# Reading the stored sums of a fast matrix product through GpSimd's transfer queue in place of SyncE's

## The chip, the core and the metric

The kernel runs on one core of a Trainium2 chip. A core has five engines with instruction streams of their own: TensorE (PE), VectorE (DVE), ScalarE (ACT), GpSimd (POOL) and SyncE (SP). Any of SP, ACT and POOL can issue transfers; the transfers themselves run on 16 DMA engines that the core's queues share. The metric is the device time of one launch in microseconds (us), lower being better.

## What is computed

One block of a streaming encoder, in float32, over 512 tokens of width 2048. The reference, cut to what matters:

```python
h = rms_norm(x, norm_gain)
proj = jnp.einsum('bsd,de->bse', h, w_in)
(sb_q, sb_k, sb_v, sb_g, gl_q, gl_k, gl_v, gl_g, gl_lr) = jnp.split(proj, offsets, axis=-1)

a_out = stick_breaking_attention(rms_norm(q) * gq, rms_norm(k) * gk, v)     # 8 heads of 128
a_out = from_heads(rms_norm(a_out) * go) * jax.nn.silu(sb_g)

log_alpha = jax.nn.log_sigmoid(gl_lr @ gla_w_alpha + gla_b_alpha) / 16
b_out = gated_linear_attention(gl_q, gl_k, gl_v, log_alpha)                # 4 heads, chunks of 64
b_out = from_heads(rms_norm(b_out) * ggo) * jax.nn.silu(gl_g)

x = x + jnp.concatenate([a_out, b_out], axis=-1) @ w_out
```

Most of the arithmetic is in the two projections, `h @ w_in` (2048 x 7184) and `mixed @ w_out` (2048 x 2048).

## The kernel before

**Products.** The projection's columns are cut into groups of 512. A float32 product is made of three matmul passes over a high and a low part of each factor (`hi`, `lo`): high by high, low by high, high by low. `split` makes the two parts of a weight tile, the high one on ACT (L177) and the low one on DVE (L178). The first two groups (q, k) are multiplied directly (`direct`). All others go two at a time through `pair`, which does seven block products in place of eight by the scheme of Strassen and Winograd: the left factor (tokens by inner dimension) is cut into two halves each way, and so are the weights. The pairs come in the order qv, vk, gqk, gv, ga, gb, o0, o1; the last two belong to `w_out`.

**The left factor.** `Acts` holds it, once for `h` (tiles named `_h`) and once for `mixed` (`_m`). Its seven forms are A11, D, NQ, S4, A12, S3 and A22, each in four slices u = 0 to 3 of the inner dimension. One slice of one form, high and low part together, is a tile of 128 partitions by 1024 numbers, 512 KB. D and S3 stay in SBUF. The other five forms are made once, written to DRAM (`_write`, L263, tiles `far_*`), and read again by `get` (L253) in every later pair, into one of four buffers (tag `as`, `NAS` = 4). There are 132 such reads: 12 in qv and 20 in each of vk, gqk, gv, ga, gb and o1. In the trace A11, A12 and A22 all bear the name `A_h` (`A_m`), NQ is `NQ_h` and S4 is `S_h`; D and S3 are kept tiles, though S3 also bears the name `S_h`.

**The four stages of a pair.** Each has four slices u. The first multiplies A11 and D (weights `st_..a`, L170, and `pw_..`). The second multiplies NQ and S4 (weight `st_..b`). The third loads two weight tiles, c and d, multiplies A12 by c and S3 by `d`, a difference that DVE makes in place (L183) and of which ACT makes the high part `hi_..d`; behind that, `gather` (L188) adds a further weight block to `pw` in SBUF by a transfer that POOL issues. The fourth splits the gathered sum (`hi_..e`) and multiplies A22 by it.

**What sets the order.** Each engine runs its instructions in program order. PE's order is written out by hand: the products of a pair with the steps of attention and of the gated part (`side.step()`) between them. The other engines' order comes from a scheduler that takes what is `urgent()` first and otherwise goes by buffers: weight tiles `st` have three buffers, `pw` four. Every weight load (L170), every read of a stored sum (L253), every write of one (L263) and every load of the residual rows `xr` (L494) is issued by SP, in one line. POOL issues the 32 gathers and does the masks of attention (L866, L873, L770). The output's residual additions are on DVE (L503, L512).

Of the kernel before, what the change touches and what calls it, by code (L numbers as in the profile page):

```python
# [7 lines left out]
F32 = mybir.dt.float32  # L8
# [85 lines left out]
def body(ctx: ExitStack, tc: tile.TileContext, x, xT, w_in, w_lr, w_alpha, vecs, w_out, out):  # L94
    nc = tc.nc
# [30 lines left out]
    def ut(name, dt=F32):  # L126

        held[0] += 1
        assert held[0] <= NU4, name
        return ring.tile([P, 2, S], dt, name=name, tag="u4", bufs=NU4)  # L130
# [10 lines left out]
    def urgent():  # L141
        return tc.high_priority(offset=URGENT)
# [47 lines left out]
    class Acts:  # L190
# [50 lines left out]
        def get(self, f, u):  # L241
            key = (f, u)
            if key in self.kept:
                return self.kept[key]
            name = f"{f}_{self.tag}{u}"
            with urgent():
                if f in self.keep:
                    t = ut(name, F32R).rearrange("p h (k t) -> p h k t", k=KU)
                    self.kept[key] = t
                else:  # L250
                    t = work.tile([P, 2, KU, H2], F32R, name=name, tag="as", bufs=NAS)
                    if key in self.far:
                        nc.sync.dma_start(t.bitcast(F32), self.far[key])  # L253
                        return t
                self._split(t, f, u)
                if f not in self.keep:
                    self._write(t, f, u, name)
            return t
# [848 lines left out]
```

## Time and profile before

| what | value |
|---|---|
| median of three runs (lowest, highest) | 921.23 us (918.57, 922.48) |
| the profiled execution: its time, its span | 920.89 us, 918.9 us |
| mean granted clock of TensorE, share of full speed | 0.966 |
| PE, DVE, ACT, POOL busy | 829.1, 665.4, 481.3, 68.4 us |
| bytes moved by transfers | 216.98 MB, 236 GB/s |

The profile is of one execution; the span runs from its first instruction to its last. Busy time leaves out the instructions that only issue transfers or wait, except on POOL, where the issue of a transfer is an instruction of its own. The granted clock is what the chip let TensorE have.

### The profile page before, as it was taken

What the parts mean: (1) busy time and instruction counts of PE and PEld (TensorE: products, weight loads), DVE (VectorE), ACT (ScalarE), POOL (GpSimd) and SP (SyncE); (2) the same over time, 40 slices, a digit from 0 to 9 for tenths busy, and PEclk for the clock granted to TensorE, in tenths of its full rate; (3) what the DMA queues carried; (4) which work ended last, traced back from release to release, by engine and by line L of the source; (5) the groups of instructions that cost most, each with busy time, mean ns of one, the idle gap of its engine ahead of it and who ended that gap; (6) DMA issues with size and microseconds to landing.
All of it is one profiled execution on the core that took longest, in us unless ns stands there. A gap on an engine that the chain in (4) does not pass through costs nothing.

```text
span 918.9 us, 11502 instructions
## 1 busy us (share of the span) xinstructions
PE 829.1 (90%) x4082; PEld 692.7 (75%) x4082; DVE 665.4 (72%) x821; ACT 481.3 (52%) x822; POOL 68.4 (7%) x113
## 2 busy tenths in 40 slices
PE   8899999899898589897999999989996989876988
PEld 5688878688787489897787788877774867665866
DVE  4542987678878987779855776778956999764654
ACT  5464566366776757564653445545734845432322
POOL 1000000100221100220100000000001000100000
PEclk9999999999999989999999999999997999897999
DMA  8878328994487524885459953887489548997695
GB/s 297 307 277 295 115 92 297 303 351 147 164 265 237 205 93 153 251 248 219 138 158 304 353 192 115 251 256 291 164 303 284 190 160 302 315 391 253 228 341 139
DMA packets 62041, 216.98 MB, mean 236 GB/s; under 512 B 7040, under 2 KB 7168, under 8 KB 61984
## 3 DMA queue, kind: packets, MB, share of 16 engines
q1 hardware_dynamic: 54928, 195.26, 59.0%
q0 software_dynamic: 4608, 16.78, 10.1%
q10 hardware_dynamic: 2448, 4.21, 1.2%
q8 instruction: 32, 0.52, 0.2%
q14 instruction: 25, 0.20, 0.1%
HBM read 191.06 MB, written 25.17 MB: 235 GB/s over the span
## 4 chain that ended last, share of the span: by engine, by line
PE 24%; DMA 13%; DVE 9%; issue 3%; ACT 2%; DVEq 0%; SPq 0%; ACTq 0%
PE x_o L111 4%; PE x_gb L111 3%; PE y_o L111 3%; PE y_gv L111 3%; PE x_gv L111 2%; DMA st_gbc<-in_w_in 2%; PE x_ga L111 2%; PE y_gb L111 2%; PE y_ga L111 2%; DMA st_o1d<-in_w_out 2%; DMA st_gad<-in_w_in 1%; DMA pw_o<-in_w_out 1%; DMA st_o0c<-in_w_out 1%; PE o L111 1%; DMA xr<-in_x 1%
## 5 line engine op out<-in xcount | busy, mean ns | idle before, releaser
L111 PE MATMUL z_q<-hi_q,A_h 128*128 128x512 f32 x128 | 35.5, 431 | 6.8 <-DVE A_h L291 3.3
L111 PEld LDWEIGHTS z_q<-hi_q,A_h 128*128 128x128 f32 x128 | 26.5, 210 | 15.4 <-DVE A_h L291 4.2
L111 PE MATMUL z_k<-hi_k,A_h 128*128 128x512 f32 x128 | 30.6, 391 | 0.0
L111 PEld LDWEIGHTS z_k<-hi_k,A_h 128*128 128x128 f32 x128 | 23.5, 188 | 4.8 <-ACT n_q L151 0.2
L178 DVE TENSOR_TENSOR lo_k<-st_k,hi_k 128x1024 fp32r<-128x1024 f32 x8 | 9.8, 1223 | 19.1 <-ACT hi_k L177 8.4
L188 POOL DMA_DIRECT2D pw_o<-in_w_out x8 | 7.0, 870 | 181.8 <-DVE st_o0d L183 73.6
L111 PE MATMUL x_gb<-hi_gbd,S_h 128*128 128x512 f32 x32 | 10.8, 493 | 8.3 <-ACT hi_gbd L177 8.3
L111 PE MATMUL y_o<-hi_o1p,D_m 128*128 128x512 f32 x32 | 9.1, 424 | 9.9 <-DVE xr L512 9.9
L111 PE MATMUL y_gqk<-D_h,hi_gqkp 128*128 128x256 f32 x64 | 10.0, 319 | 8.4 <-DVE sv L157 8.4
L188 POOL DMA_DIRECT2D pw_qv<-in_w_in x4 | 3.6, 906 | 173.2 <-DVE st_qvd L183 173.2
L111 PEld LDWEIGHTS y_gqk<-D_h,hi_gqkp 128*128 128x128 f32 x64 | 9.5, 226 | 8.8 <-DVE sv L157 8.8
L111 PE MATMUL z_q<-lo_q,A_h 128*128 128x512 f32 x64 | 15.8, 389 | 0.0
L111 PE MATMUL z_k<-lo_k,A_h 128*128 128x512 f32 x64 | 15.8, 389 | 0.0
L111 PEld LDWEIGHTS x_gb<-hi_gbd,S_h 128*128 128x128 f32 x32 | 7.4, 237 | 10.8 <-ACT hi_gbd L177 9.2
L875 ACT ACTIVATE cs_B<-cs_B 128x512 f32<-128x512 f32 x8 | 5.1, 631 | 19.9 <-POOL cs_B L873 19.9
L111 PEld LDWEIGHTS y_o<-hi_o1p,D_m 128*128 128x128 f32 x32 | 6.4, 204 | 11.6 <-DVE xr L512 10.3
L178 DVE TENSOR_TENSOR lo_q<-st_q,hi_q 128x1024 fp32r<-128x1024 f32 x8 | 9.7, 1224 | 7.4 <-ACT A_h L290 3.3
L875 ACT ACTIVATE cs_A<-cs_A 128x512 f32<-128x512 f32 x8 | 5.1, 631 | 17.2 <-POOL cs_A L873 17.2
L111 PEld LDWEIGHTS z_q<-lo_q,A_h 128*128 128x128 f32 x64 | 12.0, 188 | 2.5
L111 PEld LDWEIGHTS z_k<-lo_k,A_h 128*128 128x128 f32 x64 | 12.0, 188 | 2.5
L598 ACT ACTIVATE xt<-xt 128x1024 f32<-128x1024 f32 x8 | 8.5, 1058 | 9.3 <-DMA xt<-in_x 9.1
L111 PE MATMUL x_qv<-hi_qvd,S_h 128*128 128x512 f32 x32 | 9.8, 458 | 3.8 <-ACT hi_qvd L177 3.7
(644 smaller groups left out, 2646.0 us busy)
## 6 DMA issues: line engine op xcount, KB each, us to landing
A_h<-far_A_h SPq DMA_DIRECT2D x72, 512.0 KB, 6.1
NQ_h<-far_NQ_h SPq DMA_DIRECT2D x20, 512.0 KB, 3.8
S_h<-far_S_h SPq DMA_DIRECT2D x20, 512.0 KB, 4.1
far_A_h<-A_h SPq DMA_DIRECT2D x12, 512.0 KB, 4.4
far_A_m<-A_m SPq DMA_DIRECT2D x12, 512.0 KB, 7.7
A_m<-far_A_m SPq DMA_DIRECT2D x12, 512.0 KB, 7.7
st_q<-in_w_in SPq DMA_DIRECT2D x8, 512.0 KB, 5.1
st_k<-in_w_in SPq DMA_DIRECT2D x8, 512.0 KB, 4.8
```

The source lines that it names most:

```text
L111: nc.tensor.matmul(o, l, r, **kw)
L178: nc.vector.tensor_tensor(lo, t, hi.bitcast(F32), ALU.subtract)
L188: nc.gpsimd.dma_start(t, src, accum_op=ALU.add)
L598: nc.scalar.activation(xt, xt, AF.Square, accum_out=ss8[:, j * 2 + i:j * 2 + i + 1])
L875: nc.scalar.activation(cs, cs, AF.Exp)
```

## The change

One line: where a stored sum is read again, POOL issues the transfer in place of SP.

```diff
                     t = work.tile([P, 2, KU, H2], F32R, name=name, tag="as", bufs=NAS)
                     if key in self.far:
-                        nc.sync.dma_start(t.bitcast(F32), self.far[key])
+                        nc.gpsimd.dma_start(t.bitcast(F32), self.far[key])
                         return t
```

PE's order of instructions stays as it was. The 132 reads move from SP's row of instructions (385 before, 253 now) into POOL's (94 before, 226 now). DVE's and ACT's rows differ by a few places within a stage.

Three places show what stands where. The first is POOL in the pair vk, where masks of attention (`e_A`, `cs_B`, ...) and gathers (`pw_vk`) were, before:

```order
L866 AFFINE_SELECT e_A_1960<-e_A_1960 128x128
L873 AFFINE_SELECT cs_A_1966<-cs_A_1966 128x128
L188 DMA pw_vk_1634<-in_w_in 128x1024
L866 AFFINE_SELECT e_B_2008<-e_B_2008 128x128 x2
L873 AFFINE_SELECT cs_B_2015<-cs_B_2015 128x128 x2
L188 DMA pw_vk_1703<-in_w_in 128x1024
```

and now:

```order
L866 AFFINE_SELECT e_A_1960<-e_A_1960 128x128
L253 DMA S_h_2131<-far_S_h_1316 128x1024
L873 AFFINE_SELECT cs_A_1966<-cs_A_1966 128x128
L866 AFFINE_SELECT e_B_2008<-e_B_2008 128x128 x2
L253 DMA NQ_h_2174<-far_NQ_h_1337 128x1024
L873 AFFINE_SELECT cs_B_2015<-cs_B_2015 128x128 x2
L253 DMA A_h_2227<-far_A_h_167 128x1024
L188 DMA pw_vk_1634<-in_w_in 128x1024
L253 DMA A_h_2352<-far_A_h_271 128x1024
L253 DMA A_h_2424<-far_A_h_357 128x1024
L188 DMA pw_vk_1703<-in_w_in 128x1024
```

The reads of NQ, S4 (`S_h`) and A12 (`A_h`) of this pair now stand between the masks and the gathers; the first read of A12 is behind the mask of `cs_B`.

The second is POOL in the third and fourth stages of the pair gv, where the four gathers `pw_gv` stood one behind the other. Now there stands, from the last NQ on:

```order
L253 DMA NQ_h_4535<-far_NQ_h_1337 128x1024
L253 DMA A_h_4566<-far_A_h_167 128x1024
L188 DMA pw_gv_4141<-in_w_in 128x1024
L253 DMA A_h_4606<-far_A_h_271 128x1024
L253 DMA A_h_4646<-far_A_h_357 128x1024
L253 DMA A_h_4701<-far_A_h_443 128x1024
L188 DMA pw_gv_4186<-in_w_in 128x1024
L253 DMA A_h_4722<-far_A_h_172 128x1024
L188 DMA pw_gv_4259<-in_w_in 128x1024
L253 DMA A_h_4740<-far_A_h_276 128x1024
L188 DMA pw_gv_4310<-in_w_in 128x1024
L253 DMA A_h_4758<-far_A_h_362 128x1024
```

The first four `A_h` are the four A12, one ahead of the first gather and three behind it; of the last three `A_h`, which are A22, the third comes behind the last gather.

The third is SP at the start of the last pair, o1, where weights of the first stage (`st_o1a`, `pw_o`), stored sums (`A_m`, `NQ_m`) and residual rows (`xr`) were read, before:

```order
L170 DMA pw_o_7147<-in_w_out 128x1024
L170 DMA st_o1a_7145<-in_w_out 128x1024
L253 DMA A_m_7153<-far_A_m_6465 128x1024
L170 DMA pw_o_7186<-in_w_out 128x1024
L170 DMA st_o1a_7184<-in_w_out 128x1024
L253 DMA A_m_7192<-far_A_m_6526 128x1024
L170 DMA st_o1b_7239<-in_w_out 128x1024
L253 DMA NQ_m_7246<-far_NQ_m_6588 128x1024
L494 DMA xr_3_7059<-in_x 128x512
L494 DMA xr_0_7223<-in_x 128x512
```

and now:

```order
L170 DMA st_o1a_7106<-in_w_out 128x1024
L170 DMA pw_o_7108<-in_w_out 128x1024
L170 DMA st_o1a_7145<-in_w_out 128x1024
L263 DMA far_A_m_7041<-A_m_7038 128x1024
L170 DMA pw_o_7147<-in_w_out 128x1024
L170 DMA pw_o_7186<-in_w_out 128x1024
L170 DMA st_o1a_7184<-in_w_out 128x1024
L494 DMA xr_2_7055<-in_x 128x512
L494 DMA xr_3_7059<-in_x 128x512
L494 DMA xr_0_7223<-in_x 128x512
```

The stored sums are gone from SP's row, and the residual rows `xr_2` and `xr_3` stand right behind the last `st_o1a`.

## Rows read from the trace of the kernel before

**Rows 1.** The page: span; share of PE; transfer queues (packets, MB, share of 16 engines).

```profile
span 918.9 us, 11502 instructions
...
PE 829.1 (90%) x4082; PEld 692.7 (75%) x4082; DVE 665.4 (72%) x821; ACT 481.3 (52%) x822; POOL 68.4 (7%) x113
...
q1 hardware_dynamic: 54928, 195.26, 59.0%
q0 software_dynamic: 4608, 16.78, 10.1%
...
```

**Rows 2.** PE's waits, whole span: engine line, waited for, us in total, times, longest.

```profile
...
PE y_o L111 <- DVE xr L512: 9.9, 1, 9.9
...
PE x_gb L111 <- ACT hi_gbd L177: 8.3, 2, 6.2
...
PE x_qv L111 <- ACT hi_qvd L177: 3.7, 1, 3.7
PE x_o L111 <- ACT hi_o1d L177: 3.5, 1, 3.5
...
PE x_ga L111 <- ACT hi_gad L177: 2.5, 2, 1.8
PE x_o L111 <- DMA A_m<-far_A_m: 2.5, 1, 2.5
...
PE z_q L111 <- ACT A_h L290: 1.3, 1, 1.3
...
```

**Rows 3.** Windows of gv, ga, gb, o1: busy by engine, then PEclk, DMA share, GB/s.

```profile
...
491.00:527.00 36.00, 33.20 (x144) 26.45 (x143) 23.39 (x23) 12.88 (x13) 2.60 (x3) 1.00 1.03 351
...
593.00:632.00 39.00, 35.12 (x155) 27.96 (x155) 27.68 (x30) 20.09 (x22) 2.62 (x3) 1.00 0.88 283
...
680.00:728.00 48.00, 38.58 (x161) 30.83 (x160) 34.08 (x38) 24.97 (x30) 2.62 (x3) 0.89 0.86 275
...
877.00:919.00 42.00, 34.53 (x145) 27.74 (x143) 20.24 (x21) 10.41 (x10) 2.62 (x3) 0.95 0.76 244
...
```

**Rows 4.** PE's timeline in gb: start us, us, what, count, [idle before, releaser].

```profile
...
708.86 3.78 PE L111 MATMUL x_gb<-hi_gbd,S_h 128*128 128x512 f32 x8 [6.17 <-ACT hi_gbd L177]
...
713.67 1.98 PE L111 MATMUL y_gb<-hi_gbc,A_h 128*128 128x512 f32 x8
...
716.39 1.98 PE L111 MATMUL x_gb<-hi_gbe,A_h 128*128 128x512 f32 x8
...
```

**Rows 5.** Loads of stored sums, line 253: duration ns min/median/max; landing.

```profile
...
L253 SPq DMA_DIRECT2D A_h<-far_A_h x72: 319/372/1213, 24.6 to 716.6; - x72
...
DMA to landing us min/median/max: 3.1/5.0/11.4
...
```

**Rows 6.** Gathers, line 188: landing.

```profile
...
DMA to landing us min/median/max: 5.2/7.8/10.6
...
```

**Rows 7.** Transfer queues from 679 to 682 us: packets, MB, share of engines.

```profile
...
q0 software_dynamic: 102, 0.42, 71.1%
q1 hardware_dynamic: 95, 0.33, 30.1%
...
```

**Rows 8.** Transfer queues from 690 to 694 us.

```profile
...
q1 hardware_dynamic: 403, 1.34, 95.1%
...
```

**Rows 9.** PE's timeline in the second stage of gv.

```profile
...
470.83 1.17 PE L111 MATMUL x_gv<-lo_gvq,NQ_h 128*128 128x512 f32 x4
...
480.00 1.98 PE L111 MATMUL x_gv<-hi_gvq,NQ_h 128*128 128x512 f32 x8
...
```

**Rows 10.** Chain that ended last, around the start of the last pair.

```profile
...
824.85 8.96 DMA xr<-in_x
...
```

**Rows 11.** POOL's timeline in vk.

```profile
...
255.77 1.40 POOL L873 TENSOR_SCALAR_AFFINE_SELECT cs_B<-cs_B 128x128 f32<-128x128 f32 x2 [4.50 <-DVE cs_B L870]
...
```

**Rows 12.** PE's timeline in vk.

```profile
...
258.97 2.01 PE L111 MATMUL y_vk<-hi_vkc,A_h 128*128 128x512 f32 x8
...
```

**Rows 13.** POOL's timeline in gv.

```profile
...
509.00 0.87 POOL L188 DMA_DIRECT2D pw_gv<-in_w_in  x1 [2.81 <-issue]
...
```

## The prediction

> **What bounds the kernel now.** I read the page first. The span is 918.9 us of a profiled execution of 920.9, so 2.0 us lie around it; the median of the three runs, 921.2, is 0.3 above that execution, and a sum made against 920.9 stands for the median too. PE is the busiest engine, 829.1 us or 90% [rows 1]. A faster kernel therefore has to take from PE's 90 us of idle time, or from stretches in which PE runs at a lower clock.
>
> Second, PE's waits [rows 2]. Apart from the attention chains, which the change does not touch, three kinds stand there. The largest single one is 9.9 us for a residual addition. Then come the waits for `hi_*d`, the split of the weight difference in the third stage of a pair: 8.3 in gb, 3.7 in qv, 3.5 in o1, 2.5 in ga. A stored sum is hardly waited for at all: 2.5 us is the longest such row. So the change cannot gain by making stored sums arrive earlier. It can gain only by making something else arrive earlier.
>
> Third, the windows by stage [rows 3]: over the third and fourth stages the transfers fill 1.03 of the 16 engines in gv (491 to 527), 0.88 in ga, 0.86 in gb, 0.76 in o1. There the kernel is at or near the limit of the transfers, and the `hi_*d` waits are late weights.
>
> Fourth, what a wait costs afterwards. The twelve matmuls that begin at 708.86, behind gb's long wait, take until 713.67, 4.81 us; the next twelve take 2.72 [rows 4]. The granted clock of that window is 0.89 [rows 3], so part of it was at the lower of the two levels, 1.2 GHz. This lag of 2.1 us belongs to the wait.
>
> Fifth, the stored sums themselves: 72+20+20+12+4+4 = 132 loads of 512 KB; the row of the most frequent of them shows 372 ns on SP for an issue, and they land 3.1/5.0/11.4 us later [rows 5].
>
> **The change part by part.**
>
> *Issue.* SP loses 132 issues, about 0.37 x 132 = 49 us. That is no gain in itself: an issue by SP sits on no chain of any length. On POOL an issue of the same size (the gather) takes 0.87 us [rows 13], 132 x 0.87 = 115 us beside 68 us busy out of 919: POOL has the room. Cost 0, except where a stored sum, a gather and a mask stand in each other's way on that in-order engine (below).
>
> *How long a stored sum takes by the new way.* The trace has no plain load on POOL's queue. Below, the bound is SP's 5.0 us plus the longer issue (0.87 - 0.37 = 0.5): 5.5. Above, it is the gather's 5.2/7.8/10.6 [rows 6]; the gather reads and adds at the target, so it moves more. I take 6. Room in the dense second stage: a buffer is free when its product ends and is wanted three products later, in gv from 472.00 (470.83 + 1.17) to 480.00, 8.0 us [rows 9]. So 6 fits, with 2 us left, and the dense stages cost nothing; at 8 they begin to cost.
>
> *Weights with fewer loads ahead of them (gain).* In the third stage SP's queue holds c, d and the stored sums of A12 in one line. Taken out, they leave c and d a queue of their own. When both queues have work, the transfer engines serve both: in 679 to 682 the POOL queue took 71.1% and SP's 30.1% [rows 7]. But bytes are the same, so a stage can win only what its transfers leave free. I give nothing where the share is about 1 (gv; I take qv to be like it), and half of the waits in gb, ga and o1: gb 8.3 + 2.1 lag, ga 2.5, o1 3.5, together 16.4, half is **-8**. Bounds: 0 and -20.1, all four waits and the lag (16.4 + 3.7).
>
> The Trainium skill, "DMA: Bandwidth & Descriptors", section "Queues, rings and completion order", says that each transfer engine takes turns between the rings it has work for, packet by packet. That agrees with 679 to 682; by it alone c and d would get at least half the engines at once, and the gain would be near the upper bound. It does not fit 690 to 694, where SP's queue had 95.1% although two gathers had been issued [rows 8].
>
> *The residual rows (gain).* The longest wait ends with an x load that SP issued at 824.85, just when another load had landed, and that took 8.96 us [rows 10]. In the new order no stored sum stands ahead of it in SP's queue. Its transfer still shares the engines. I take a third, **-3**; bounds 0 and -9.9.
>
> *The start (gain).* SP's first stored sum goes out at 24.6 [rows 5], among the loads of the first projection; without it the small low-rank weights come a place earlier. The wait for the first split after that is 1.3 us [rows 2]. **-1**; bounds 0 and -1.3.
>
> *A12 behind the first gather (loss).* In gv's new POOL order the second A12 stands behind the first gather, which occupies POOL for 0.87 us and the queue for longer. About 0.5 us in each of gv, gb, ga and o1: **+2**; bounds 0 and +6.
>
> *A22 behind the last gather (loss).* The third and fourth A22 of gv now stand behind the last gather in the queue; that gather can take 10.6 us to land [rows 6], and before they went by SP past it. About 0.4 us in each of five pairs: **+2**; bounds 0 and +8.
>
> *Masks ahead of stored sums in vk (loss).* POOL's row now has the first A12 of vk behind the mask of cs_B, which ended at 257.17 (255.77 + 1.40) [rows 11]. Landing 5 us later is 262.2; PE used that A12 at 258.97 [rows 12]. If the mask comes when it did, that is 3 us late. DVE has the scan ahead of that mask a few places earlier now, so I take **+1**; bounds 0 and +5. The masks that a stored sum now delays have PE idle or busy with other work behind them: 0.
>
> *DVE and ACT* change only by places within a stage: 0, hidden under PE's products; if that cover were gone, about 1 us (one split).
>
> Sum: -8 - 3 - 1 + 2 + 2 + 1 = -7. 920.9 - 7 = **914**.
>
> **Rivals.**
>
> *Larger gain.* SP's weights get their half of the engines at once and all `hi_*d` waits fall: -20 - 3 - 1 + 5 = -19, **902**. For it: the alternation in 679 to 682. Against it: 1.03 in gv; there no order of loads gives back anything. Chance 0.15.
>
> *No change.* The kernel waits for bytes, not for an order; the stored sums only change places with the weights, and gains and losses cancel: **921**. For it: 1.03 and 0.88 of the engines in use, and the 0.37 us issues on no path. The Trainium skill, "DMA: Bandwidth & Descriptors", section "Issuing engines are not separate DMA queues", says that loads of whichever issuing engine run on the same 16 engines, and only issue time is saved; by that the time stays where it is. The trace agrees with the shared engines; no run here shows that the order does nothing. Against it: the longest waits are for what stands behind stored sums. Chance 0.24.
>
> *Slower: stored sums come late.* A queue of POOL is served late when SP's is full (690 to 694 [rows 8]). If stored sums then land like gathers, between 7.8 and 10.6 for the later half, each of these is about 1.2 us over the 8.0 us of room. Of the 48 A12 and A22 loads of the six pairs from vk to o1, half are 24, and if half of the lateness adds to the span, 24 x 1.2 / 2 = +14: **935**, with no gain from c and d. It decides from a landing of 8 us on. A heavier form of it: the POOL queue's packets took 10.1% for 16.78 MB against 59.0% for 195.26 [rows 1], twice as much per MB; if that were the queue and not the addition, 69 MB more would take 21% of the engines more than now, which three saturated stages of 36 us or so would feel as some 8 us each. For it: the gather's slow first packets. Against it: gathers add at the target. Chance 0.24.
>
> **How the numbers follow.** Forecast 914 (906 to 919) with chance 0.37; larger gain 0.15; no change 0.24; slower 0.24. The three runs spread by 0.2% to each side, so about 0.5% can be told from none. Below 916.6: nearly all of the first (0.34) and the second, 0.49; within 0.5%, 0.27; above 925.8, 0.24. The range leaves one in ten at each end: below 898 half the larger gain and a little more, above 933 the upper half of the slower case.
>
> **What would show it.** Right: the rows PE <- `hi_gbd`, `hi_gad`, `hi_o1d` fall by half and the clock of the gb window rises; the x load lands before 832; stored sums land at a median near 6 us and PE hardly waits for them. Wrong: rows PE <- DMA `far_*` of more than some 6 us in all, a landing median of 8 us, gathers landing at over 11 us with waits for `hi_*e`, or POOL masks that PE waits for.

## The result, and the profile after

The changed kernel takes 945.8 us (median of four runs, 941.2 to 946.5), the kernel before 920.6 beside it: a ratio of 1.026, 95% interval 1.022 to 1.030, so 25 us slower. The forecast was 914, with 898 to 933 as range. The profiled execution is one of 941.2.

The page of the changed kernel: its span, the busy time of the engines, the two transfer queues (packets, MB, share of 16 engines).

```profile
span 939.4 us, 11517 instructions
...
PE 841.8 (90%) x4082; PEld 699.5 (74%) x4082; DVE 663.5 (71%) x821; ACT 483.3 (51%) x822; POOL 137.1 (15%) x245
...
q1 hardware_dynamic: 35920, 126.04, 36.9%
q0 software_dynamic: 23616, 85.99, 30.7%
...
```

Beside [rows 1] the queue of POOL now moves 86.0 MB and SP's 126.0. PE is busy for 841.8 us in place of 829.1 with the same 4082 matmuls: 12.7 of the 20.5 us that this span is longer are matmuls that ran longer, and the mean granted clock has gone from 0.966 to 0.949. Only the rest, 7.8 us, is added idle time.

The stored sums themselves, the view of line 253 in the changed kernel (issues with their ns; who waited for them; us from issue to landing):

```profile
...
L253 POOL DMA_DIRECT2D A_h<-far_A_h x72: 527/541/886, 10.1 to 737.8; - x72
...
who waited for it (us, times):
  PE y_gb L111: 0.8, 1
  PE y_gqk L111: 0.2, 1
...
DMA to landing us min/median/max: 3.4/5.2/12.7
...
```

They land as fast as before (5.2 at the median, 5.0 in [rows 5]), the issue on POOL takes 0.54 us, and PE waits for them for 1.0 us in all, 4.5 before. Whatever costs 25 us, PE does not spend it in waiting for a stored sum.

PE's waits in the changed kernel (waited for, us, times, longest):

```profile
...
PE y_o L111 <- DVE xr L512: 7.7, 1, 7.7
PE y_gb L111 <- DVE lo_gbb L178: 4.9, 1, 4.9
PE x_gv L111 <- DVE gv L445: 4.7, 1, 4.7
PE x_qv L111 <- DVE lo_qve L178: 4.2, 1, 4.2
PE x_o L111 <- ACT hi_o0d L177: 4.0, 1, 4.0
PE x_gb L111 <- DVE z L445: 3.9, 1, 3.9
...
PE x_gv L111 <- DVE lo_gve L178: 3.4, 1, 3.4
...
PE x_ga L111 <- DVE lo_gae L178: 2.5, 1, 2.5
...
PE x_qv L111 <- ACT hi_qvd L177: 2.2, 1, 2.2
...
PE x_ga L111 <- ACT hi_gad L177: 1.8, 2, 1.1
...
PE x_o L111 <- ACT hi_o1d L177: 0.3, 1, 0.3
...
```

Of [rows 2] the waits for `hi_gbd` and, but for 0.3, `hi_o1d` are gone, and the one for xr is 7.7 in place of 9.9. But names stand here now that were not among the long waits before: `gv` and `z`, which are evacuations (DVE reads a finished product out of PE's accumulator), and `lo_*b` and `lo_*e`, DVE's low parts of splits. DVE's own waits for weights say why. First the kernel before, then the changed one (instruction, waited for, us, times, longest):

```profile
...
DVE st_gvd L183 <- DMA st_gvd<-in_w_in: 8.7, 3, 3.5
...
DVE st_gbd L183 <- DMA st_gbd<-in_w_in: 3.7, 2, 3.3
...
DVE pw_vk L183 <- DMA pw_vk<-in_w_in: 1.4, 2, 1.1
...
DVE pw_ga L183 <- DMA st_gaa<-in_w_in: 0.4, 1, 0.4
...
```

```profile
...
DVE st_gbd L183 <- DMA st_gbd<-in_w_in: 19.1, 4, 8.5
DVE st_gvd L183 <- DMA st_gvd<-in_w_in: 12.1, 3, 6.8
...
DVE pw_vk L183 <- DMA pw_vk<-in_w_in: 8.7, 1, 8.7
...
DVE pw_ga L183 <- DMA pw_ga<-in_w_in: 7.8, 1, 7.8
...
```

DVE stands still for 19.1 us at the sum `st_gbd` where it stood for 3.7, and for 8.7 at `pw_vk` where it stood for 1.4. These are the sums of weights on L183, and DVE works in order: while one waits for its weight, what is queued behind it waits too. That costs time only where PE needs what stands behind.

The same place in gv in both kernels, DVE's timeline (start, us, what, [idle before, releaser]); before:

```profile
...
490.70 1.41 DVE L445 SCALAR_TENSOR_TENSOR gv<-x_gv,nrstd,gvy 128x512 f32<-128x512 f32 x2 [0.94 <-PE x_gv L111]
495.57 1.23 DVE L183 TENSOR_TENSOR st_gvd<-pw_gv,st_gvd 128x1024 f32<-128x1024 f32 x1 [3.46 <-DMA st_gvd<-in_w_in]
...
```

After:

```profile
...
503.70 1.22 DVE L183 TENSOR_TENSOR st_gvd<-pw_gv,st_gvd 128x1024 f32<-128x1024 f32 x1 [6.84 <-DMA st_gvd<-in_w_in]
504.84 1.40 DVE L445 SCALAR_TENSOR_TENSOR gv<-x_gv,nrstd,gvy 128x512 f32<-128x512 f32 x2
...
```

Before, DVE evacuates x_gv first (`gv`, 490.70) and then waits 3.46 us for the weight of the sum. Now the sum stands first, waits 6.84 us for its weight, and the evacuation starts at 504.84, behind it. PE adds the next product to the same accumulator, so it waits too, and then runs slowly; PE's timeline of the changed kernel there:

```profile
...
505.64 3.78 PE L111 MATMUL x_gv<-hi_gvd,S_h 128*128 128x512 f32 x8 [4.66 <-DVE gv L445]
509.22 1.52 PE L111 MATMUL x_gv<-lo_gvd,S_h 128*128 128x512 f32 x4
510.58 1.78 PE L111 MATMUL y_gv<-hi_gvc,A_h 128*128 128x512 f32 x7
...
```

The wait is 4.66 us; the twelve matmuls behind it take from 505.64 to 510.58, 4.94 us, where twelve take 2.72 otherwise [rows 4].

Windows of the third and fourth stages of gv and of gb in the changed kernel, the columns as in [rows 3]:

```profile
...
498.00:545.00 47.00, 38.87 (x148) 30.71 (x147) 25.20 (x24) 13.92 (x14) 6.93 (x11) 0.85 0.90 294
...
706.00:750.00 44.00, 37.59 (x162) 30.12 (x161) 31.51 (x35) 23.21 (x27) 5.38 (x8) 0.92 0.81 266
...
```

In gv these stages take 47 us where they took 36, the transfers fill 0.90 of the engines where it was 1.03, and the clock is 0.85 where it was 1.00. In gb they take 44 where they took 48, and the clock has risen from 0.89 to 0.92: there PE's first long wait, 4.9 us for `lo_gbb`, now lies ahead of the window, in the second stage.

### The profile page after: what moved, and what is told of

The parts are those of the page before. It is cut to its first block, busy times and chain, and to the rows that moved or that the text cites. A ratio compares the mean times of both kernels' runs of the same rounds, so it can differ in the third digit from the quotient of the medians.

```text
span 939.4 us, 11517 instructions
## 1 busy us (share of the span) xinstructions
PE 841.8 (90%) x4082; PEld 699.5 (74%) x4082; DVE 663.5 (71%) x821; ACT 483.3 (51%) x822; POOL 137.1 (15%) x245
## 3 DMA queue, kind: packets, MB, share of 16 engines
q1 hardware_dynamic: 35920, 126.04, 36.9%
## 4 chain that ended last, share of the span: by engine, by line
PE 43%; DMA 22%; DVE 20%; issue 9%; ACT 3%; POOL 2%; DVEq 0%; SPq 0%; POOLq 0%; ACTq 0%
PE x_o L111 4%; PE z_q L111 4%; PE y_o L111 3%; PE x_gv L111 3%; DMA st_gbd<-in_w_in 3%; PE y_gqk L111 3%; PE x_ga L111 3%; PE x_gqk L111 3%; PE y_gv L111 3%; PE x_qv L111 3%; PE y_ga L111 2%; PE y_qv L111 2%; DMA st_o1d<-in_w_out 2%; DMA st_qvd<-in_w_in 2%; PE x_gb L111 1%
## 5 line engine op out<-in xcount | busy, mean ns | idle before, releaser
L253 POOL DMA_DIRECT2D A_h<-far_A_h x72 | 43.0, 601 | 279.1 <-DMA far_S_h<-S_h 98.4
L253 POOL DMA_DIRECT2D S_h<-far_S_h x20 | 10.7, 537 | 80.8 <-PE x_gqk L111 20.8
L253 POOL DMA_DIRECT2D NQ_h<-far_NQ_h x20 | 10.7, 536 | 69.1 <-PE x_gb L111 12.9
L183 DVE TENSOR_TENSOR st_gbd<-pw_gb,st_gbd 128x1024 f32<-128x1024 f32 x4 | 4.9, 1226 | 19.1 <-DMA st_gbd<-in_w_in 19.1
L111 PEld LDWEIGHTS y_gqk<-D_h,hi_gqkp 128*128 128x128 f32 x64 | 9.5, 226 | 10.2 <-DVE sv L157 10.2
L814 ACT ACTIVATE jq_q<-n_q 128x128 f32<-128x128 f32 x32 | 9.9, 310 | 11.5 <-DVE n_q L445 9.8
L977 ACT ACTIVATE ge<-z 128x1024 f32<-128x1024 f32 x8 | 8.5, 1060 | 13.1 <-DVE z L973 13.1
L111 PE MATMUL x_gv<-hi_gvd,S_h 128*128 128x512 f32 x32 | 9.7, 454 | 4.7 <-DVE gv L445 4.7
```

The source lines that it names most:

```text
L111: nc.tensor.matmul(o, l, r, **kw)
L183: (eng or nc.vector).tensor_tensor(o, a, b, op)
L253: nc.gpsimd.dma_start(t.bitcast(F32), self.far[key])
L814: nc.scalar.activation(junk, t[:, a, h * P:(h + 1) * P], AF.Square, accum_out=ss[:, j * 4 + h:j * 4 + h + 1])
L977: nc.scalar.activation(e, z, AF.Exp, scale=-1.0)
```

## The experiments

The change does two things that can be told apart: it moves 132 reads to another queue, and the scheduler, given another queue, puts the instructions of DVE, ACT and SP in a slightly different order. To part them, most experiments give an engine's order from a table of instruction numbers, by an edge between neighbours that orders issue and makes nothing wait for a result:

```diff
     with tile.TileContext(nc) as tc:
-        body(tc, *args, o)
+        body(tc, *args, o); pin(tc, PINNED)
...
+def pin(tc, orders):
+    by = {i.name: i for i in tc.nc.cur_bb.bb.instructions}
+    for row in orders:
+        row = [by[f"I-{n}"] for n in row if f"I-{n}" in by]
+        for a, b in zip(row, row[1:]):
+            tc.add_manual_dep(b, a.name, mybir.DependencyInfo(mybir.DependencyClass.NoSync, ...))
```

`PINNED` holds a row for each engine whose order is given; the others are left to the scheduler. Ratios are to the kernel before on the same chip, with 95% intervals. The theories are Q (the second queue takes transfer engines from the weights), S (the order that the scheduler makes) and P (POOL's line: gathers, masks and stored sums stand behind each other).

**The two parts.** e1: the changed kernel, `PINNED` = DVE, ACT and SP as before, POOL as in the change.

> The stored sums are read by POOL as in the change, but DVE, ACT and SP keep the order of instructions that they had before (POOL has the order of the change). Theory Q (the second queue takes a share of the transfer engines from the weights): stays slow, 935 to 947, with DVE's waits for st_*d and pw_* weights well above the 70 us of before. Theory S (the scheduler's new order on DVE, ACT and SP is what costs): back to 917 to 925, DVE's weight waits as before. Theory P (gathers stand behind stored sums on POOL): stays slow, and PE's waits are for hi_*e and lo_*e behind gathers issued late.

938.4 us, 1.020 (1.013 to 1.027). e2: as e1, with SP's row of the change.

> As e1, but SP has the order of the change as well (residual rows xr ahead of the weights st_gbd, weights in the new order); DVE and ACT keep the order of before. Theory Q: same as e1 within 4 us. Theory S: if SP's order is what costs, 5 to 12 us slower than e1, in gb and at the start of o1; if DVE's and ACT's, as e1. Theory P: as e1.

947.5 us, 1.029 (1.025 to 1.034): with DVE's old order, SP's new row costs some 9 us more, though the intervals overlap. e3: the kernel before (line 253 on SP), `PINNED` = DVE, ACT and SP (without stored sums) as in the change.

> The stored sums are read by SP as before, but DVE, ACT and SP (but for the stored sums) have the order of instructions of the change. Theory Q: within 6 us of before, 918 to 927. Theory S: slow as the change, 938 to 947. Theory P: as before, 918 to 925.

932.5 us, 1.012 (1.008 to 1.016). Neither theory holds alone: the order costs some 12 us with the old queue, and the new queue some 18 with the old order. But e1 has a fault of its own. Its POOL row was made for another order of DVE, and PE's waits in e1 show it:

```profile
...
PE y_vk L111 <- DMA A_h<-far_A_h: 4.9, 1, 4.9
PE T_k L115 <- DVE w_A L155: 4.6, 1, 4.6
...
```

The first A12 of vk stood behind a mask that DVE now fed later; the wait is the 0 to 5 us that the prediction bounded for that place. So e1 says too much against the queue.

e4: as e1, but with POOL's row merged from the times at which the trace of before shows each mask, gather and stored sum issued.

> As e1 (stored sums by POOL, DVE, ACT and SP in the order of before), but POOL's own row is merged by the times at which the trace of before shows each thing ready: a stored sum stands ahead of a mask or a gather that became ready after it, and behind those that were ready earlier. So nothing on POOL waits behind something that comes later. Theory P (what the queue costs is POOL's single line: masks and stored sums behind each other): 917 to 925, and the waits of vk and gqk that e1 had (y_vk <- A_h 4.9, T_k <- w_A 4.6) gone. Theory Q (weights lose a share of the transfer engines): as e1, 933 to 941.

926.5 us, 1.009 (1.006 to 1.013), and of the two waits of e1 `y_vk <- A_h` is gone while `w_A` keeps 3.2. About half of what e1 lost was POOL's line; the other half is not. e5: the kernel before with DVE and ACT as in the change.

> Stored sums by SP as before; DVE and ACT in the order of the change; SP's order is left to the scheduler. Theory S in its form for DVE and ACT (sums of weights for later products stand ahead of splits and evacuations that PE wants first): as e3, 929 to 935, with the waits vka (n_q) and lo_gve, lo_qve. Theory S in its form for SP (xr ahead of st_gbd): 918 to 925, and y_gb <- lo_gbb gone.

932.0 us, 1.012 (1.007 to 1.018): as e3. That points to DVE and ACT, but does not clear SP, whose row was left to the scheduler and is in gb neither that of before nor that of the change. The next run keeps SP's row as before.

**Which instructions.** e6: the kernel before, all engines as before but for three instructions on DVE. In order, as the rows of DVE differ:

```diff
+L183 TENSOR_TENSOR st_gvd_4594<-pw_gv_4186,st_gvd_4594
 L445 SCALAR_TENSOR_TENSOR gv_0_4549<-x_gv_4137,nrstd,gvy_4531
 L445 SCALAR_TENSOR_TENSOR gv_0_4549<-x_gv_4138,nrstd,gvy_4533
-L183 TENSOR_TENSOR st_gvd_4594<-pw_gv_4186,st_gvd_4594
...
+L183 TENSOR_TENSOR pw_ga_4799<-pw_ga_4799,st_gaa_4797
 L445 SCALAR_TENSOR_TENSOR gv_0_4715<-y_gv_4135,rstd,gvm_4347
 L445 SCALAR_TENSOR_TENSOR gv_0_4715<-y_gv_4136,rstd,gvm_4349
 L178 TENSOR_TENSOR lo_gve_4755<-pw_gv_4259,hi_gve_4754
-L183 TENSOR_TENSOR pw_ga_4799<-pw_ga_4799,st_gaa_4797
...
+L183 TENSOR_TENSOR pw_ga_5006<-pw_ga_5006,st_gaa_5004
 L157 TENSOR_SCALAR gv_1_4790<-x_gv_4138,rstd
 L178 TENSOR_TENSOR lo_gaa_4853<-st_gaa_4848,hi_gaa_4852
 L178 TENSOR_TENSOR lo_gap_4893<-pw_ga_4850,hi_gap_4892
-L183 TENSOR_TENSOR pw_ga_5006<-pw_ga_5006,st_gaa_5004
```

> The kernel before (stored sums by SP, every engine's order as before) with three DVE instructions moved to where the change has them, all in the pair gv and its passage to ga: one st_gvd sum ahead of the evacuation gv of x_gv, and the sums of pw_ga for u = 0 and u = 3 ahead of evacuations of gv and of the splits lo_gaa and lo_gap. Theory S (DVE's line is held by a sum that waits for a weight): +7 to +12 us, 926 to 932, with PE x_gv <- gv 4 to 5 us and y_ga <- gv about 4. If these places are not the cause: 917 to 922.

931.1 us, 1.012 (1.009 to 1.015): three instructions of 821 on one engine, moved by two or three places, cost 11 us or 1.2%, as much as the whole new orders of e3 and e5. Its timelines show it. DVE at the first place and at the third:

```profile
...
495.96 1.23 DVE L183 TENSOR_TENSOR st_gvd<-pw_gv,st_gvd 128x1024 f32<-128x1024 f32 x1 [6.94 <-DMA st_gvd<-in_w_in]
497.11 1.40 DVE L445 SCALAR_TENSOR_TENSOR gv<-x_gv,nrstd,gvy 128x512 f32<-128x512 f32 x2
...
```

```profile
...
537.87 1.23 DVE L183 TENSOR_TENSOR pw_ga<-pw_ga,st_gaa 128x1024 f32<-128x1024 f32 x1 [4.02 <-DMA st_gaa<-in_w_in]
539.02 0.74 DVE L157 TENSOR_SCALAR gv<-x_gv,rstd 128x512 f32<-128x512 f32 x1
...
```

PE's waits in e6, and its timeline behind the first:

```profile
...
PE x_gv L111 <- DVE gv L445: 4.7, 1, 4.7
...
PE y_ga L111 <- DVE gv L157: 3.1, 1, 3.1
...
```

```profile
...
497.91 3.78 PE L111 MATMUL x_gv<-hi_gvd,S_h 128*128 128x512 f32 x8 [4.75 <-DVE gv L445]
...
503.19 2.25 PE L111 MATMUL y_gv<-hi_gvc,A_h 128*128 128x512 f32 x8
...
```

Two waits of 4.7 and 3.1 us; and behind the first, twelve matmuls take 5.28 us in place of 2.72.

e10: the changed kernel, each engine in the order of the change, with these three put back.

> The changed kernel (stored sums by POOL, every engine's order as the change has it) with the three sums of weights of e6 put back on DVE to where they stood before: st_gvd behind the evacuation gv, the two pw_ga behind the evacuations and splits. Theory S: what e6 lost comes back, 930 to 938, and x_gv <- gv is gone. If the change's loss lies mainly elsewhere and these three places only matter with the queue of before: 941 to 947.

936.6 us, 1.020 (1.015 to 1.025): 9 us of the 25 come back by the medians. The two intervals just overlap (the change's begins at 1.022), but the traces show the loss at its place. Start of the first matmul of gv and of the second stage of ga, which lie around the three sums (us, one execution each):

| | before | e6 | the change | e10 |
|---|---|---|---|---|
| gv, first stage (`hi_gva`) | 438.0 | 436.9 | 444.6 | 449.5 |
| ga, second stage (`hi_gaq`) | 560.9 | 571.5 | 579.1 | 573.8 |
| between | 122.9 | 134.6 | 134.5 | 124.3 |

The three sums add 11.7 us in the old queue, and putting them back takes 10.2 out of the change. e13: e3 with the three put back.

> As e3 (stored sums by SP, DVE, ACT and SP in the order of the change) with the three sums of weights of e6 put back. Theory S in its narrow form (these three places are the whole cost of the new order): 918 to 924. In its wide form (the sums of pw_vk and the places in gb and o1 cost as well): 925 to 931.

921.5 us, 1.004 (1.000 to 1.007). With the old queue, the rest of the new order, SP's row included, costs some 3 us. e15: e10 with the sums of `pw_vk` for u = 0, 1 and 3 (qv to vk) put back as well.

> As e10, with the three sums of pw_vk in the passage from qv to vk put back on DVE as well. If these hold up n_q and lo_qve at a cost to the end: 929 to 934. If the following stage has the time for it (the lag of 5 us in e5 was given back by 4 within the pair): as e10, 934 to 939.

932.5 us, 1.015 (1.010 to 1.019). The waits `x_qv <- lo_qve` (4.2 in the change, 1.1 in e10) and `y_vk <- n_q` (3.2 in e10) are gone. The median is 4 below e10's, but the intervals overlap; these sums may cost some 4 us.

**Which stored sums.** e7 and e8 are e4 with a part of the forms on each queue (e8 with the tuple `("A11", "NQ", "S4")`):

```diff
-                        nc.gpsimd.dma_start(t.bitcast(F32), self.far[key])
+                        (nc.gpsimd if f in ("A12", "A22") else nc.sync).dma_start(t.bitcast(F32), self.far[key])
```

> As e4 (orders of before, POOL's row merged by readiness), but only A12 and A22 are read by POOL; A11, NQ and S4 stay with SP. Theory Q (sharing of the transfer engines with the weights c and d): the 8.6 us of e4 stay here, 923 to 930. Theory P (POOL's line beside attention's masks, in the dense stages): 917 to 922.

> As e4, but only A11, NQ and S4 are read by POOL; A12 and A22 stay with SP. Theory Q: 916 to 921, as before. Theory P: 921 to 928.

e7: 927.5 us, 1.008 (1.005 to 1.011). e8: 919.2 us, 0.998 (0.995 to 1.001). The 76 reads of the first two stages cost nothing on POOL; the 56 of the third and fourth carry all of e4's loss. e14: e10 with A12 and A22 read by SP.

> As e10 (the change with the three sums put back), with A12 and A22 read by SP again, so that POOL reads A11, NQ and S4 alone. Theory Q (A12 and A22 on a queue of their own take from the weights c and d): the 7 us of e7 come back, 925 to 932. Otherwise as e10, 934 to 939.

921.8 us, 1.004 (1.001 to 1.007): with the three sums back and these two forms back, the changed kernel is within 0.4% of the kernel before. DVE still waits 17.1 us at `st_gbd` there, where it waited 19.1 in the change and 3.7 before: that longest row, which comes with the new order, costs little.

e16: e10 with POOL's row merged by the times at which e14's trace shows each thing issued.

> As e10 (the change with the three sums put back; all stored sums by POOL), with POOL's row merged by readiness: the times at which the trace of e14 shows each gather, mask and stored sum ready set their order, so that none stands behind one that becomes ready later. Theory P (gathers and masks held behind stored sums on POOL's line): 920 to 928, most of the 15 us between e10 and e14 gone. Theory Q (A12 and A22 on a second queue delay the weights c and d, whatever their place on POOL): 932 to 938. In between: both, by the share that goes.

932.3 us, 1.015 (1.012 to 1.019), between e10 (936.6) and e14 (921.8): some 4 us are POOL's line, though the intervals of e16 and e10 overlap, and 10 are the second queue for A12 and A22, the rest of POOL's row being in e14's order. The landing of gv's d weights, by tile, in e14 and in e16 (us, min/median/max):

```profile
...
DMA to landing us min/median/max: 4.6/5.9/8.0
...
```

```profile
...
DMA to landing us min/median/max: 4.8/6.8/7.9
...
```

The medians of the eight pairs' d weights are all higher in e16, by 0.1 to 0.9 us, 0.6 in the mean (those of the c weights by 0.2 in the mean, and not all). There are 32 loads of d; if each delayed its stage by that much it would be 19 us, and half of it is what is missing. DVE's waits at the sums `st_*d` add up to 59.1 us in e14 and 70.4 in e16.

One place shows it with little else that differs, the first `st_gbd` with the first A12 of gb behind it. In e14 SP issues both, and DVE waits for the weight:

```profile
...
668.28 0.33 SPq L170 DMA_DIRECT2D st_gbd<-in_w_in  x1
...
671.36 0.33 SPq L253 DMA_DIRECT2D A_h<-far_A_h  x1
...
676.44 1.23 DVE L183 TENSOR_TENSOR st_gbd<-pw_gb,st_gbd 128x1024 f32<-128x1024 f32 x1 [6.35 <-DMA st_gbd<-in_w_in]
...
```

In e16 POOL issues the A12:

```profile
...
677.87 0.33 SPq L170 DMA_DIRECT2D st_gbd<-in_w_in  x1
...
680.50 0.53 POOL L253 DMA_DIRECT2D A_h<-far_A_h  x1 [2.19 <-PE x_gb L111]
...
687.84 1.22 DVE L183 TENSOR_TENSOR st_gbd<-pw_gb,st_gbd 128x1024 f32<-128x1024 f32 x1 [8.26 <-DMA st_gbd<-in_w_in]
...
```

The A12 goes out 3.1 and 2.6 us behind the weight, at about the same moment. With it behind the weight in one queue DVE waits 6.35 us, with it in a queue of its own 8.26.

**Two tries at something faster.** e9: the kernel before, orders kept, residual rows by POOL.

```diff
-            nc.sync.dma_start(t, x[j * P:(j + 1) * P, self.g * S:(self.g + 1) * S])
+            nc.gpsimd.dma_start(t, x[j * P:(j + 1) * P, self.g * S:(self.g + 1) * S])
```

> The kernel before, all orders kept and the stored sums by SP, but the 16 loads of the residual rows go by POOL's queue. If the 9.9 us wait of y_o for xr is SP's line (the load issued late), it falls to under 3 us and the time to 911 to 917. If it is the transfer engines, it stays and the time is 917 to 922.

925.4 us, 1.006 (1.002 to 1.009): slower by 0.6%. The wait for xr is 6.9, and the wait `x_ga <- lo_gae` has grown from 1.3 to 5.3. e11: the kernel before with one row moved on SP, and e12: the same in e8.

```diff
 L170 DMA pw_o_7108<-in_w_out 128x1024
+L494 DMA xr_3_7059<-in_x 128x512
 L263 DMA far_A_m_7041<-A_m_7038 128x1024
...
 L253 DMA NQ_m_7246<-far_NQ_m_6588 128x1024
-L494 DMA xr_3_7059<-in_x 128x512
```

> The kernel before with one residual row (xr_3 of the passage from o0 to o1) issued by SP 12 places earlier, ahead of the last write of a stored sum. If SP's order set the 9.9 us wait of y_o for xr: that wait under 3 us, and 911 to 917. If the row's buffer is not free by then, SP's line stands still: 920 to 928.

> e8 (A11, NQ and S4 by POOL, A12 and A22 by SP, orders of before) with the residual row of e11 moved as well. If both help: 908 to 915; if e11's row only shifts a wait: 916 to 921.

e11: 918.1 us, 1.000 (0.996 to 1.003). e12: 918.4 us, 0.998 (0.994 to 1.002). SP's timeline in e11, and PE's wait:

```profile
...
812.92 0.33 SPq L494 DMA_DIRECT2D xr<-in_x  x1
...
```

```profile
...
PE y_o L111 <- DVE xr L512: 7.2, 1, 7.2
...
```

The load now goes out at 812.92, 12 us earlier than in [rows 10], and PE still waits 7.2 us for the addition: it stands on DVE behind sums of `pw_o`, which wait for their own weights. No version here beats the kernel before by more than can be told.

## Why the prediction was wrong, step by step

**The step that failed first** is "*DVE and ACT* change only by places within a stage: 0". The places were seen and, at worst, priced by the length of one instruction. Nor do they stay within a stage: the first of the three sums belongs to the third stage of gv and passes the evacuation that ends the second, the other two belong to ga and pass evacuations of gv. Their price is that of a wait: a sum that needs a weight still on its way holds all that stands behind it. Three of them cost 6 to 11 us: 11 by e6 alone, 10 at their place in the traces of the change and e10, 9 by the medians of these two, 6 by their ratios (2.6 less 2.0%). With them back, what remains of the new order costs some 3 in the old queue (e13).

**The second step that failed** is the gain of 8 us for weights "with fewer loads ahead of them". The rows from which it was summed did fall: the waits for `hi_gbd`, `hi_gad` and `hi_o1d` went from 14.3 us to 2.1. Most of that is the new order and no gain: in e13, with the old queue, `hi_gbd` and `hi_o1d` are gone too, and PE waits 5.7 us for `lo_gbb`, which stands behind a sum on DVE (4.9 in the change). With the orders of before the queue brings the three rows down to 10.7 us (e4) and 9.6 (e7), a part of the gain that was hoped for. It loses more elsewhere: the kernel is 7 us slower in e7, and about 10 in the change's own order (e16 against e14: 932.3 and 921.8). A queue of its own does not only take the stored sums from in front of the weights. In one line a read of A12 or A22 comes behind the weights issued earlier. In a second line it moves beside them. The DMA view of the changed kernel from 690 to 696 us, while the weight `st_gbd`, issued at 688.20, is on its way (packets, MB, share):

```profile
...
q0 software_dynamic: 357, 1.32, 53.9%
q1 hardware_dynamic: 481, 1.07, 46.3%
...
```

POOL's queue, with a read of NQ (issued at 688.00) and the first A12 (690.72), has 53.9% of the engines, SP's, which carries what DVE waits for, 46.3%; the sum that needs that weight starts at 698.40, after 8.49 us of DVE's waiting. Not all of that wait is POOL's doing: SP's new row has four loads of residual rows ahead of this weight, and in e14, with the same row and A12 behind the weight, 6.35 remain. The Trainium skill, "DMA: Bandwidth & Descriptors", section "Queues, rings and completion order", has the engines take turns between the rings by packet, and these shares agree. That this sharing makes all of the 10 us between e14 and e16 is argued from this place, the waits and the landing times, each read in one execution; no run took the sharing alone away.

**The other terms.** The stored sums landed at 5.2, not 6, and the dense second stages cost nothing, as forecast (e8). The slower rival's mechanism, stored sums that come late, is refuted by the 1.0 us for which PE waits for them; its side was right, and its loss of 14 is smaller than the measured 25. Its heavier form, a queue that takes more of the engines for each byte, is refuted too: SP's queue lost 69.2 MB and 195.5 us of the 16 engines' time (59.0% of 918.9 less 36.9% of 939.4), and POOL's gained the same 69.2 MB and 195.6 us. "No change" failed as well: the order of the same transfers is worth 1.15% (e14 and e16). The loss for A12 and A22 behind gathers (2 and 2) is of the size of what e16 gives back, 4 us, though this is POOL's line as a whole: gathers stand behind stored sums that wait for a buffer as well. The mask of vk (bounds 0 and 5) was a wait of 4.9 in e1 and of nothing in the change, where DVE's scan stands earlier. The xr term was -3; the wait fell by 2.2, though the load went out at 840.92 and took 11.53 us, more than the 8.96 before, and e11 shows that the load was not what held the wait in the end. The 1.3 us wait at the start is gone, as forecast.

**The signs.** Most of what the prediction named as signs of being right came true: the three `hi_*d` rows together fell by more than half, the clock of gb's window rose from 0.89 to 0.92, stored sums landed at 5.2 and PE hardly waited for them. Only the x load landed at 852.5 (840.92 and 11.53), not before 832. None of its signs of being wrong appeared. All of them are waits for the transfers that it had in mind; none looks at DVE's own waits, where the sums of weights stood still for 69.3 us in all before and for 140.0 after. That sum alone tells no price either (it is 112.8 in e14, at 0.4%): what counts is what stands behind each wait.

**The account.** By ratios, each with the uncertainty of its run: e14 0.38%, the queue of A12 and A22 1.15% more (e16), POOL's line 0.44% more (e10), the three sums 0.63% more (the change), 2.60% in all. The intervals reach 0.3 to 0.5% to each side. By them alone only the second step stands clear of its neighbours; the last rests on e6 and on the traces as well.

## What to carry to other kernels

When a scheduler orders an engine, a transfer moved to another queue moves instructions on engines that the diff does not touch: look for an instruction that waits for a transfer and now stands ahead of one that PE waits for, and price it at the transfer's remaining time and the slow matmuls behind the wait, not at its own length. A wait that has left the list of the busiest engine may have moved: sum up the waits of the engines that feed it too. And a load that nobody is waiting for may be better off in the same queue, behind those that are waited for: here 56 of them in a queue of their own cost 7 to 10 us, most likely because they then take a share of the engines while the others are on their way.

## What was not expected of the hardware

A wait of 4 to 5 us costs PE more than its length: twelve matmuls behind it took 4.94 us (after a wait of 4.66) and 5.28 (after 4.75) in place of 2.72. The prediction had read one such lag, but not that slower matmuls outweigh the added waits: over the changed kernel they ran 12.7 us longer in all, of the 20.5, and that stands in no list of waits. The plain load's instruction took 0.54 us on POOL, less than the gather's 0.87 from which it was priced.
